# The first norm of a hybrid decoder layer: another way to start TensorE, another split of the first loads, and a small load issued later

## The chip, the core and the metric

The kernel runs on one core of one Trainium2 chip. The metric is the device time of one execution in microseconds (us); lower is better. The engines are TensorE (PE, with its weight loads shown apart as PEld), VectorE (DVE), ScalarE (ACT), GpSimd (POOL) and SyncE (SP). SP, ACT and POOL each have a queue from which they issue DMA transfers. Every engine works its own instructions off in order and waits on semaphores for the others.

## The reference, cut to what matters

One layer on x of shape (1, 512, 1024), all float32:

```
h    = rmsnorm(x, attn_norm_g)              # per row: x / sqrt(mean(x*x) + 1e-6) * g
proj = h @ w_in                             # 1024 -> 5144 columns: attention q, k, v, RWKV-7 inputs, gates
o_a  = nsa_mixer(...)                       # compressed, selected and windowed attention, 8 heads
o_b  = rwkv7_mixer(...)                     # recurrence over 512 tokens, 8 heads of 64
x    = x + (sigmoid(ga) * (o_a @ w_proj_a) + sigmoid(gb) * (o_b @ w_proj_b)) @ w_out
x    = x + conv_ffn(rmsnorm(x, ffn_norm_g)) # 1024 -> 2 x 2816 -> 1024
```

The compressed attention branch maps blocks of 32 tokens by a small two-layer network: `gelu(flat @ cmp_w1) @ cmp_w2`, once for keys (k) and once for values (v). `cmp_w1` is 2048 x 256, `cmp_w2` is 256 x 64.

## The kernel before

Every large product is computed from two float32r parts of each operand: a weight tile `raw` is loaded by SP's queue (line 267, 512 KB each as a rule, three buffers in turn), ACT rounds it to `whi` (`act`, line 124), DVE or POOL writes the rest `wlo` (line 296), and TensorE runs three products for each block of 128 inputs: hi\*hi, hi\*rest, rest\*hi (`mm`, line 121). The activations are kept the same way, as `hh` and `hl`, with channels on the partitions.

**The first norm** (lines 145 to 374) makes `hh` and `hl` from x. Its order on PE, ACT, DVE and POOL is written out by hand.

- x stands in four tiles `xt[:, t]` of 128 rows by 1024. SP issues their four loads first (line 153). ACT issues the load of the identity matrix (`ident`, in the tile `kc`, line 154) and of the norm's gains (`pr0`, line 155), POOL the loads of eight small parameter vectors into `pra` (line 162). Between, ACT takes one square root of a constant, which loads its table.
- PE runs 16 transposes of `ident` that nothing reads (line 329, `NWARM = 16`).
- For each tile t: ACT squares the row and sums it, ACT and DVE make the reciprocal root (`rstd1`, five small steps), DVE scales the tile into `hs[t]` (line 131). The last tile is scaled in two halves of 512 columns. PE then transposes the tile in blocks of 128 x 128 (`turn`, line 335) into eight PSUM banks `pts[k]`, one for each block k of channels; tile 2 leaves its last block, and tile 3 all of its blocks, to the loop below.
- After tile 1's transposes PE also transposes `pr0` and `pra` (lines 349 and 350) into a corner of bank 7. ACT copies the gains out as `ang`, DVE copies the rest as `prm` (line 353) and makes `omm = 1 - mu` from it.
- ACT rounds the first weight tile to `hi` before `ang`. POOL then writes one column of `omm` into `lo` (line 355), and after that the true `lo` in two halves (line 357). POOL's one-column copy is overwritten; it only makes POOL wait for `omm`.
- A loop over k transposes the rest of bank k, ACT writes `hh[:, k]` from it (a copy with a scale), and DVE writes `hl[:, k]`.
- The first product `p0` follows. Its bank is one of the four that `pts[0]` to `pts[3]` use, so it waits until DVE has read `pts[0]`.

**The compression** (function `compress`) runs in steps between the chunks of the RWKV recurrence, whose order on PE and SP is written out by hand; a scheduler orders ACT and DVE there. Each of four steps `s4` takes two tiles of `cmp_w1`, k and v, and multiplies them into `hx`. When `s4 == 1` is done SP issues the two loads of `cmp_w2` into `cw2` (line 805, 64 KB each, in rows of 256 bytes). `cw2` is read some steps later, by the second layer. In SP's queue these two loads stand between the loads of `cmp_w1` for `s4 == 2`, ahead of a tile of `w_in` and of the last k tile of `cmp_w1` (into `AB`).

Of the kernel before, what the change touches and what calls it, by code (L numbers as in the profile page):

```python
# [11 lines left out]
F32 = mybir.dt.float32  # L12
F32R = mybir.dt.float32r
I32 = mybir.dt.int32
AF = mybir.ActivationFunctionType
# [6 lines left out]
D = 1024  # L22
NT = S // 128
# [18 lines left out]
ROWS = {}  # L42
# [39 lines left out]
def hybrid_block(ctx: ExitStack, tc: tile.TileContext, A: dict, out: bass.AP):  # L82
    nc = tc.nc
    v, sc, te = nc.vector, nc.scalar, nc.tensor
    NWARM = 16

    def dbg(name, ap):
        if name in DBG:
# [2 lines left out]
    x_in = A["x"][0]  # L91
# [28 lines left out]
    def mm(o, l, r, start, stop):  # L120
        te.matmul(o, lhsT=l, rhs=r, start=start, stop=stop)  # L121

    def act(o, i, f=AF.Copy, **kw):
        sc.activation(o, i, f, **kw)  # L124
# [4 lines left out]
    def ts(o, a, s1, s2, op0=ALU.mult, op1=ALU.add):  # L129
        if s2 is None:  # L130
            v.tensor_scalar(o, a, s1, None, op0=op0)
        else:
            v.tensor_scalar(o, a, s1, s2, op0=op0, op1=op1)
# [6 lines left out]
    ident, mask, ones, cmask = kc[:, 0:128], kc[:, 128:256], kc[:, 256:384], kc[:, 384:416]  # L140
# [3 lines left out]
    xp_cm, xp = pool("x")  # L144
    xt = xp.tile([128, NT, D], F32, name="xt")
    eps1 = xp.tile([128, 1], F32, name="eps1")
    v.memset(eps1, 1e-6)
    one = xp.tile([128, 1], F32, name="one")
    v.memset(one, 1.0)
    act(one, one, AF.Sqrt)  # L150
    pr0 = xp.tile([8, 128], F32, name="pr0")
    for t in range(NT):
        nc.sync.dma_start(xt[:, t], x_in[128 * t:128 * t + 128])
    sc.dma_start(ident, A["consts"][:, 0:128])
    sc.dma_start(pr0, A["attn_norm_g"][0].rearrange("(r p) -> r p", p=128))
    pra = xp.tile([NR0, 128], F32, name="pra")
    for name in ("rwkv_mu", "rwkv_w0", "rwkv_a0", "rwkv_k_k", "rwkv_k_a", "rwkv_r_k", "rwkv_ln_g", "rwkv_ln_b"):
        r0, n = ROWS[name]
# [4 lines left out]
    ang = cp.tile([128, 8], F32, name="ang")  # L163
# [5 lines left out]
    def cols(name):  # L169
        r0, n = ROWS[name]  # L170
        return prm[:, r0:r0 + n]
# [154 lines left out]
    with tc.manual_schedule(engines={getattr(mybir.EngineType, e) for e in ("PE", "Activation", "DVE", "Pool")}):  # L326
        pts = [mmb() if k < 4 else pa() if k < 6 else pb() for k in range(KT)]
        for i in range(NWARM):
            te.transpose(pts[7][:, 384:512], ident, ident)
        hi = wp.tile([128, KT, 128], F32R, name="whi", tag="whi", bufs=2)  # L330
        lo = wp.tile([128, KT, 128], F32R, name="wlo", tag="wlo", bufs=2)
        raw = loads.pop(0)[0]

        def turn(t, k):
            te.transpose(pts[k][:, 128 * t:128 * t + 128], hs[t][:, 128 * k:128 * k + 128], ident)

        for t in range(NT):
            r = ssx[:, t:t + 1]
            act(hs[t], xt[:, t], AF.Square, accum_out=r)
            rstd1(r)  # L340
            for c0 in ((0, 512) if t == NT - 1 else (0,)):
                c1 = 512 + c0 if t == NT - 1 else D
                ts(hs[t][:, c0:c1], xt[:, t, c0:c1], r, None)
            if t < NT - 1:
                for k in range(KT - t // 2):
                    turn(t, k)
            if t == 1:
                pt = pts[7][:, 384:512]
                te.transpose(pt[:, 0:8], pr0, ident[0:8, 0:8])
                te.transpose(pt[:, 8:8 + NR0], pra, ident[0:NR0, 0:NR0])  # L350
        act(hi, raw)
        act(ang, pt[:, 0:8])
        v.tensor_copy(prm[:, 0:NR0], pt[:, 8:8 + NR0])
        ts(omm, cols("rwkv_mu"), -1.0, 1.0)
        nc.gpsimd.tensor_copy(lo[:, 0, 0:1], omm[:, 0:1])
        for i in (slice(0, 4), slice(4, 8)):
            nc.gpsimd.tensor_tensor(lo[:, i], raw[:, i], hi[:, i].bitcast(F32), op=ALU.subtract)
        late.append(nc.gpsimd.tensor_copy)
        wsplit()
        for k in range(KT):  # L360
            for t in range(NT - 1 - k // 7, NT):
                turn(t, k)
            act(hh[:, k], pts[k], AF.Copy, scale=ang[:, k:k + 1])
            stt(hl[:, k], pts[k], ang[:, k:k + 1], hh[:, k].bitcast(F32), ALU.mult, ALU.subtract)
        ts(w0h, cols("rwkv_w0"), 0.5, None)
        ts(kah, cols("rwkv_k_a"), 0.5, None)
        ts(a0h, cols("rwkv_a0"), 0.5, None)
        ts(oma, cols("rwkv_k_a"), -0.5, 1.0)
        p0 = mmb()
        for k in range(KT):  # L370
            mm(p0, hi[:, k], hh[:, k], k == 0, False)
            if k:
                mm(p0, lo[:, k - 1], hh[:, k - 1], False, False)
            mm(p0, hi[:, k], hl[:, k], False, False)
        mm(p0, lo[:, KT - 1], hh[:, KT - 1], False, True)
# [403 lines left out]
    def compress():  # L779
        Rk = [sg1[:, 2 * a:2 * a + 2].rearrange("p m s -> p (m s)").rearrange("p (j g n) -> p j g n", j=16, g=2)  # L780
              for a in range(2)]
        for a, s_ in enumerate("kv"):
            v.memset(Rk[a][:, :, :, 31:32], 0.0)
            r0 = ROWS["cmp_pe_" + s_][0]
            for g in range(2):
                dv = Dc[:, a, g].rearrange("p (n j) -> p j n", j=8)
                for jh in range(2):
                    tt(Rk[a][:, 8 * jh:8 * jh + 8, g, 0:31], dv[:, :, jh:31 + jh],
                       prm[:, r0 + 8 * jh:r0 + 8 * jh + 8, None].to_broadcast([128, 8, 31]), ALU.add)
        cw2, hid, hidT, kcd = (QK[:, o:o + 256] for o in range(3072, 4096, 256))  # L790
        cw2 = cw2.rearrange("p (a m d) -> p a m d", a=2, m=2)
        hidT = hidT.rearrange("p (m a n) -> p m a n", m=2, a=2)
        kcd = kcd[0:32].rearrange("p (g a d) -> p g a d", g=2, a=2)
        kcs = cp.tile([32, 2], F32, name="kcs")
        yield
        hx = mmb()[:, 0:256]
        for s4 in range(4):
            w = [wnext(4, 256) for _ in range(2)]
            for j in range(4):
                for a in range(2):  # L800
                    mm(hx[64 * a:64 * a + 64], Rk[a][:, 4 * s4 + j].rearrange("p g n -> p (g n)"), w[a][:, j],
                       s4 + j == 0, s4 + j == 6)
            if s4 == 1:
                for a, s_ in enumerate("kv"):
                    nc.sync.dma_start(cw2[:, a], A["cmp_w2_" + s_][0].rearrange("(m p) d -> p m d", p=128))
            yield
        act(hid, hx, AF.Square)
        ts(hid, hid, 0.044715, 1.0)
        tt(hid, hid, hx, ALU.mult)
        act(hid, hid, AF.Tanh, scale=math.sqrt(2.0 / math.pi))  # L810
        stt(hid, hid, 1.0, hx, ALU.add, ALU.mult)
        yield
        pt = mmb()
        for m in range(2):
            te.transpose(pt[:, 128 * m:128 * m + 128], hid[:, 128 * m:128 * m + 128], ident)
        act(hidT.rearrange("p m a n -> p (m a n)"), pt[:, 0:256])
        yield
        kc_ps = mmb()
        for g in range(2):
            for m in range(2):  # L820
                mm(kc_ps[0:32, 64 * g:64 * g + 64], hidT[:, m, 0, 32 * g:32 * g + 32], cw2[:, 0, m], m == 0, m == 1)
        nc.gpsimd.memset(vcb, 0.0)
        for g in range(2):
            for e in range(2):
                bs = slice(64 * g + 32 * e, 64 * g + 32 * e + 32)
                for m in range(2):
                    mm(kc_ps[bs, 128:192], hidT[:, m, 1, 32 * g:32 * g + 32], cw2[:, 1, m], m == 0, m == 1)
        for g in range(2):
            for e in range(2):
                bs = slice(64 * g + 32 * e, 64 * g + 32 * e + 32)  # L830
                act(vcb[bs, 2 * g + e], kc_ps[bs, 128:192], AF.Copy, scale=0.5)
        for g in range(2):
            act(kcd[:, g, 0], kc_ps[0:32, 64 * g:64 * g + 64], AF.Copy, scale=0.5)
            act(kcd[:, g, 1], kcd[:, g, 0], AF.Square, accum_out=kcs[:, g:g + 1])
        rstd(kcs, DH)
        for g in range(2):
            ts(kcd[:, g, 1], kcd[:, g, 0], kcs[:, g:g + 1], None)
            ts(kcd[:, g, 0], kcd[:, g, 0], kcs[:, g:g + 1], None)
        yield
        pt = mmb()  # L840
        for g in range(2):
            te.transpose(pt[:, 32 * g:32 * g + 32], kcd[:, g].rearrange("p a d -> p (a d)"), ident[0:32, 0:32])
        ptv = pt[:, 0:64].rearrange("p (g n) -> p g n", g=2)
        act(KC[:, :, 0], ptv, AF.Copy, scale=kg)
        stt(KC[:, :, 1], ptv, kg, KC[:, :, 0].bitcast(F32), ALU.mult, ALU.subtract)
# [530 lines left out]
```

## Time and profile before

| | us |
|---|---|
| runs | 837.89, 836.97, 837.40 |
| median of the runs | 837.40 |
| the profiled execution's own time | 838.0 |
| its span, first instruction to last | 836.2 |
| PE busy in the span | 822.0 |
| DVE, ACT, POOL busy | 515.8, 407.2, 51.5 |

The profile is that of one execution. Its times count from the first instruction; 1.8 us of the execution's own time lie outside the span. A row of the timeline gives the start, the duration and the engine of an instruction or of several equal ones in a row, the line of the kernel, and what is written from what; in square brackets stands how long the engine sat idle before it and what released it. L124, L121, L131, L133 and L136 are lines of one-line helpers (`act`, `mm`, `ts` without and with an addend, and `stt`), so such rows are told apart by their tiles. "Idle before" is shown only where there was some. The granted clock is 1.00 in every stretch that the profile lists, so the pace of TensorE in the first microseconds is read from the spacing of its rows.

### The profile page before, as it was taken

How to read it: one execution, taken by the hardware profiler on the slowest of the kernel's cores; microseconds unless marked ns; L12 is line 12 of the kernel's file. 1: busy time of each engine (PE TensorE's matmuls, PEld its weight loads, DVE VectorE, ACT ScalarE, POOL GpSimd, SP SyncE). 2: the span in 40 equal slices, each digit the busy share in tenths (PEclk: the TensorE clock that was granted, in tenths of full speed). 3: DMA queues.
4: the chain of work that ended last, by engine and by line, in shares of the span. 5: the costliest groups of instructions: out<-in, count | busy, mean ns of one | idle time of the engine just before them, and what ended most of it. 6: DMA issues, size and time to landing. Idle time of an engine off the chain costs nothing.

```text
span 836.2 us, 12860 instructions
## 1 busy us (share of the span) xinstructions
PE 822.0 (98%) x5091; PEld 668.2 (80%) x5091; DVE 515.8 (62%) x1003; ACT 407.2 (49%) x794; POOL 51.5 (6%) x68
## 2 busy tenths in 40 slices
PE   7999999999999999999999999999999999999998
PEld 6777778887778886777788988888888888888886
DVE  5477779974565878787665665566655566322222
ACT  6766654453455777676334454444444444221220
POOL 6200020140000100011000000000000000000000
PEclk9999999999999999999999999999999999999999
DMA  7432222346372310000275033333333332223421
GB/s 233 112 81 70 76 76 77 79 117 185 102 127 77 83 45 14 26 27 26 67 251 174 1 101 100 101 102 88 92 98 101 100 101 97 85 97 114 139 75 51
DMA packets 109264, 78.73 MB, mean 94 GB/s; under 512 B 3869, under 2 KB 97876, under 8 KB 109204
## 3 DMA queue, kind: packets, MB, share of 16 engines
q1 hardware_dynamic: 106800, 73.92, 30.6%
q10 hardware_dynamic: 1060, 2.55, 1.0%
q0 software_dynamic: 1344, 1.45, 0.8%
q8 instruction: 40, 0.66, 0.3%
q14 instruction: 20, 0.16, 0.1%
HBM read 74.56 MB, written 2.29 MB: 92 GB/s over the span
## 4 chain that ended last, share of the span: by engine, by line
PE 53%; DVE 0%; DVEq 0%; issue 0%
PE ps_mm L121 52%; PE ps_a L200 0%; PE ps_b L200 0%; PE ps_a L121 0%; PE ps_b L1180 0%; PE ps_mm L1180 0%; DVE x L127 0%; DVEq L1372 0%; PE ps_a L1132 0%
## 5 line engine op out<-in xcount | busy, mean ns | idle before, releaser
L121 PE MATMUL ps_mm<-hh,whi 128*128 128x512 f32 (+1 forms) x624 | 242.4, 391 | 1.4 <-DVE hl L136 0.8
L296 DVE TENSOR_TENSOR wlo<-raw,whi 128x1024 fp32r<-128x1024 f32 (+1 forms) x111 | 131.5, 1185 | 180.0 <-PE ps_mm L121 157.8
L121 PE MATMUL ps_mm<-hl,whi 128*128 128x512 f32 (+1 forms) x624 | 240.2, 387 | 0.0
L124 ACT ACTIVATE whi<-raw 128x1024 fp32r<-128x1024 f32 (+3 forms) x124 | 123.3, 996 | 155.9 <-PE ps_mm L121 142.1
L121 PE MATMUL ps_mm<-hh,wlo 128*128 128x512 f32 (+1 forms) x624 | 152.1, 384 | 0.0
L121 PEld LDWEIGHTS ps_mm<-hh,whi 128*128 128x128 f32 x624 | 117.2, 188 | 28.2 <-ACT whi L124 1.5
L121 PEld LDWEIGHTS ps_mm<-hl,whi 128*128 128x128 f32 x624 | 117.4, 188 | 23.0 <-issue 1.0
L121 PEld LDWEIGHTS ps_mm<-hh,wlo 128*128 128x128 f32 x624 | 115.1, 188 | 23.5
L121 PE MATMUL ps_mm<-whi,aT 128*128 128x512 f32 x352 | 84.5, 390 | 0.0
L121 PEld LDWEIGHTS ps_mm<-whi,aT 128*128 128x128 f32 x352 | 65.9, 188 | 14.3 <-issue 0.4
L136 DVE SCALAR_TENSOR_TENSOR cgv<-ps_mm,cw,cgv 128x511 f32<-128x511 f32 (+1 forms) x88 | 65.4, 746 | 1.6
L124 ACT ACTIVATE cgv<-ps_mm,cw 128x512 f32<-128x512 f32 x44 | 34.2, 780 | 23.3 <-PE ps_mm L121 23.3
L121 PE MATMUL ps_mm<-wlo,aT 128*128 128x512 f32 x176 | 44.3, 389 | 0.0
L124 ACT ACTIVATE P<-P,nm 128x512 f32<-128x512 f32 (+3 forms) x64 | 35.4, 553 | 15.0 <-DVE nm L1154 14.9
L124 ACT ACTIVATE aT<-cgv 128x512 fp32r<-128x512 f32 x22 | 13.9, 632 | 56.8 <-DVE cgv L127 56.8
L121 PEld LDWEIGHTS ps_mm<-wlo,aT 128*128 128x128 f32 x176 | 33.0, 188 | 6.9
L124 ACT ACTIVATE cgv<-cgv 128x512 f32<-128x512 f32 x22 | 13.9, 632 | 41.0 <-DVE cgv L136 41.0
L296 POOL TENSOR_TENSOR wlo<-raw,whi 128x512 fp32r<-128x512 f32 (+3 forms) x13 | 20.5, 1577 | 203.2 <-PE ps_mm L121 148.8
L1154 DVE CUSTOM_DVE_ANT_0 P<-ps_a,AB 128x512 f32<-128x512 f32 (+3 forms) x64 | 29.4, 484 | 4.2 <-PE ps_a L121 3.7
L127 DVE TENSOR_TENSOR x<-x,ps_mm 128x512 f32<-128x512 f32 (+1 forms) x17 | 11.1, 656 | 24.4 <-PE ps_mm L121 23.2
L127 DVE TENSOR_TENSOR aT<-cgv,aT 128x512 fp32r<-128x512 f32 x22 | 15.3, 693 | 14.7 <-ACT aT L124 14.7
L121 PE MATMUL ps_a<-KH,qst 128*128 128x512 f32 (+3 forms) x64 | 21.4, 349 | 1.6 <-DVE nm L1154 0.9
(354 smaller groups left out, 1202.1 us busy)
## 6 DMA issues: line engine op xcount, KB each, us to landing
raw<-in_w_up_dram SPq DMA_DIRECT2D x44, 512.0 KB, 3.8
raw<-in_w_in_dram SPq DMA_DIRECT2D x38, 512.0 KB, 4.1
raw<-in_w_down_dram SPq DMA_DIRECT2D x22, 512.0 KB, 3.6
raw<-in_w_out_dram SPq DMA_DIRECT2D x8, 512.0 KB, 4.1
xt<-in_x_dram SPq DMA_DIRECT2D x4, 512.0 KB, 5.3
raw<-in_cmp_w_v_dram SPq DMA_DIRECT2D x4, 512.0 KB, 3.9
raw<-in_w_proj_b_dram SPq DMA_DIRECT2D x8, 256.0 KB, 2.7
raw<-in_w_proj_a_dram SPq DMA_DIRECT2D x8, 256.0 KB, 2.7
```

The costliest lines, as they stand in the source:

```text
L121: te.matmul(o, lhsT=l, rhs=r, start=start, stop=stop)
L124: sc.activation(o, i, f, **kw)
L127: v.tensor_tensor(o, a, b, op=op)
L136: v.scalar_tensor_tensor(o, a, s, b, op0=op0, op1=op1)
L296: eng.tensor_tensor(lo, raw, hi.bitcast(F32), op=ALU.subtract)
L1154: v.tensor_tensor_reduce(out=P[:, i], in0=sp[:, N * (i - i0):N * (i - i0) + N], in1=BT[:, h, 384 - 128 * qt:512], scale=-1.0, scalar=-NEG, ...
```

## The change

- PE's start: a tile `warm` of 128 x 128 ones, filled by DVE, is multiplied with itself 15 times (plain float32 matmuls through `mm`) in place of the 16 transposes of `ident`.
- The first loads: the rows of tiles 0 and 1 are split in two halves of 64, SP loads the upper, ACT the lower. `ident` follows on ACT's queue behind its two halves, and `pr0` behind the square root. The order on ACT and SP is now written out by hand here too.
- The last tile is scaled in columns 0 to 255 and 256 to 1023.
- ACT makes `ang` ahead of `hi`. `omm` is made from the PSUM bank in place of `prm`. POOL's copy of `omm` into `lo` is gone.
- The compression issues the loads of `cw2` after step 2 in place of step 1. In SP's queue they stand now behind the `w_in` tile and behind the last k tile of `cmp_w1`.

In the built program PE's order is otherwise the same but for six matmuls of the second product, which come out in a slightly different order of hi and rest. At one place of the recurrence the scheduler now puts, on ACT, the rounding of a weight tile (`whi`) ahead of a gate (`sg`) and of the recurrence's `UV`; on DVE `wlo` now stands ahead of its copy to `UV`. Nothing else moves.

```
-    NWARM = 16
+    NWARM = 15
...
-    act(one, one, AF.Sqrt)
+    warm = xp.tile([128, 128], F32, name="warm")
+    v.memset(warm, 1.0)
     pr0 = xp.tile([8, 128], F32, name="pr0")
-    for t in range(NT):
-        nc.sync.dma_start(xt[:, t], x_in[128 * t:128 * t + 128])
-    sc.dma_start(ident, A["consts"][:, 0:128])
-    sc.dma_start(pr0, A["attn_norm_g"][0].rearrange("(r p) -> r p", p=128))
+    with tc.manual_schedule(engines={mybir.EngineType.Activation, mybir.EngineType.SP}):
+        for t in range(2):
+            nc.sync.dma_start(xt[0:64, t], x_in[128 * t:128 * t + 64])
+            sc.dma_start(xt[64:128, t], x_in[128 * t + 64:128 * t + 128])
+        for t in range(2, NT):
+            nc.sync.dma_start(xt[:, t], x_in[128 * t:128 * t + 128])
+        sc.dma_start(ident, A["consts"][:, 0:128])
+        act(one, one, AF.Sqrt)
+        sc.dma_start(pr0, A["attn_norm_g"][0].rearrange("(r p) -> r p", p=128))
...
         for i in range(NWARM):
-            te.transpose(pts[7][:, 384:512], ident, ident)
+            mm(pts[7][:, 384:512], warm, warm, True, True)
...
             act(hs[t], xt[:, t], AF.Square, accum_out=r)
             rstd1(r)
-            for c0 in ((0, 512) if t == NT - 1 else (0,)):
-                c1 = 512 + c0 if t == NT - 1 else D
+            cut = (0, 256, D) if t == NT - 1 else (0, D)
+            for c0, c1 in zip(cut, cut[1:]):
                 ts(hs[t][:, c0:c1], xt[:, t, c0:c1], r, None)
...
                 te.transpose(pt[:, 0:8], pr0, ident[0:8, 0:8])
                 te.transpose(pt[:, 8:8 + NR0], pra, ident[0:NR0, 0:NR0])
+        act(ang, pt[:, 0:8])
         act(hi, raw)
-        act(ang, pt[:, 0:8])
         v.tensor_copy(prm[:, 0:NR0], pt[:, 8:8 + NR0])
-        ts(omm, cols("rwkv_mu"), -1.0, 1.0)
-        nc.gpsimd.tensor_copy(lo[:, 0, 0:1], omm[:, 0:1])
+        r0, n = ROWS["rwkv_mu"]
+        ts(omm, pt[:, 8 + r0:8 + r0 + n], -1.0, 1.0)
         for i in (slice(0, 4), slice(4, 8)):
             nc.gpsimd.tensor_tensor(lo[:, i], raw[:, i], hi[:, i].bitcast(F32), op=ALU.subtract)
...
-            if s4 == 1:
+            if s4 == 2:
                 for a, s_ in enumerate("kv"):
                     nc.sync.dma_start(cw2[:, a], A["cmp_w2_" + s_][0].rearrange("(m p) d -> p m d", p=128))
```

## The prediction

> **What bounds the kernel now.** I read the page's busy times first, then the timeline of the first 15 us engine by engine, then TensorE's waits, and last the one stretch behind the norm in which a wait of TensorE meets the second edit.
>
> ```profile
> span 836.2 us, 12860 instructions
> PE 822.0 (98%) x5091; PEld 668.2 (80%) x5091; DVE 515.8 (62%) x1003; ACT 407.2 (49%) x794; POOL 51.5 (6%) x68
> ```
>
> TensorE is busy for 822.0 of 836.2 us, so nearly all that is left to win is the 14.2 us in which it is idle, and what it does at a slow pace or for nobody. The timeline of TensorE up to the first product:
>
> ```profile
> 4.85 3.67 PE L329 MATMUL ps_b<-kc 128*128 128x128 f32 x16 [4.85 <-DMA kc<-in_consts_dram]
> 8.31 1.06 PE L335 MATMUL ps_mm<-kc,h 128*128 128x128 f32 x4
> ...
> 10.02 1.06 PE L335 MATMUL ps_mm<-kc,h 128*128 128x128 f32 x4
> 10.87 0.42 PE L335 MATMUL ps_a<-kc,h 128*128 128x128 f32 x2
> ...
> 11.44 0.23 PE L349 MATMUL ps_b<-kc,pr 8*128 8x8 f32 x1
> ...
> 11.79 0.66 PE L335 MATMUL ps_mm<-kc,h 128*128 128x128 f32 x4
> ...
> 12.61 0.60 PE L335 MATMUL ps_mm<-kc,h 128*128 128x128 f32 x4
> ...
> 14.50 0.50 PE L121 MATMUL ps_mm<-hh,whi 128*128 128x512 f32 x1 [0.75 <-DVE hl L136]
> ```
>
> The reader is to see three things. The warm-up waits 4.85 us for the identity. It ends at 8.31. And the pace changes: 16 transposes from 4.85 to 8.31 are 0.216 us each, four from 10.02 to 10.87 still 0.21, but tile 2's seven from 11.79 to 12.61 take 0.117. So TensorE came to its full pace at about 10.9, 6.0 us after its first instruction, and most of the norm's transposes ran at half pace. From 14.50 on it hardly stops; what is won ahead of 14.50 should reach the end. The other engines in the same stretch:
>
> ```profile
> 4.65 1.06 ACT L124 ACTIVATE h<-xt 128x1024 f32<-128x1024 f32 x1 [1.95 <-DMA xt<-in_x_dram]
> ...
> 8.84 1.06 ACT L124 ACTIVATE h<-xt 128x1024 f32<-128x1024 f32 x1
> ...
> 10.03 0.29 ACT L124 ACTIVATE rx_y<-ssx,eps 128x1 f32<-128x1 f32 x1
> 10.43 1.06 ACT L124 ACTIVATE whi<-raw 128x1024 fp32r<-128x1024 f32 x1
> 11.89 0.18 ACT L124 ACTIVATE ang<-ps_b 128x8 f32<-128x8 f32 x1 [0.40 <-PE ps_b L350]
> 12.98 0.69 ACT L124 ACTIVATE hh<-ps_mm,ang 128x512 fp32r<-128x512 f32 x1 [0.91 <-PE ps_mm L335]
> ```
>
> ```profile
> 6.80 0.75 DVE L131 TENSOR_SCALAR h<-xt,ssx 128x1024 f32<-128x1024 f32 x1
> ...
> 8.17 0.75 DVE L131 TENSOR_SCALAR h<-xt,ssx 128x1024 f32<-128x1024 f32 x1
> ...
> 9.55 0.75 DVE L131 TENSOR_SCALAR h<-xt,ssx 128x1024 f32<-128x1024 f32 x1
> ...
> 11.00 0.88 DVE L131 TENSOR_SCALAR h<-xt,ssx 128x512 f32<-128x512 f32 x2
> 12.10 0.20 DVE L353 COPY prm<-ps_b 128x42 f32<-128x42 f32 x1 [0.22 <-ACT ang L124]
> ...
> 13.70 0.75 DVE L136 SCALAR_TENSOR_TENSOR hl<-ps_mm,ang,hh 128x512 fp32r<-128x512 f32 x1 [1.18 <-ACT hh L124]
> ```
>
> The scaled tiles 0, 1 and 2 are ready at 7.55, 8.92 and 10.30, the first half of tile 3 at 11.44. TensorE begins on tile 0 at 8.31, on tile 2 at 11.79, on tile 3 at 12.61: it is late for each. ACT waits for it 0.40 and 0.91 us, DVE then 1.18. TensorE's slow pace sets the start of `hh`, and by `hl` the start of the first product.
>
> **The start of TensorE.** The fill of `warm` is one DVE instruction of 128 columns, less than the 0.44 us of half a tile's scaling, so the first warm matmul starts at some 1.2 us. What a float32 matmul costs is seen here:
>
> ```profile
> 54.16 1.02 PE L121 MATMUL ps_a<-kk,kc 128*128 128x512 f32 x2
> 55.03 0.59 PE L121 MATMUL ps_a<-tv,kc 128*128 128x512 f32 x1
> ```
>
> One of 512 columns occupies 0.87 us, so 128 columns take 0.22 at full pace and 0.43 at half. Fifteen at half pace last 6.5 us, to 7.7; with the full pace after the same 6.0 us as before (at 7.2) they end at 7.5. Tile 0 is ready at 7.55. So the warm-up costs 0 to 0.15 us there, and the transposes run at 0.117: tile 0 to 8.6, tile 1 from 8.92 to 9.9, then the two small transposes, 0.35 from 11.44 to 11.79 before. These need the last of POOL's parameter loads:
>
> ```profile
> 4.97 0.51 POOL L162 DMA_DIRECT2D pra<-in_rwkv_ln_b_dram  x1
> ...
> 12.58 0.19 POOL L355 CAST wlo<-omm 128x1 fp32r<-128x1 f32 x1 [6.82 <-DVE omm L133]
> 12.85 1.27 POOL L357 TENSOR_TENSOR wlo<-raw,whi 128x512 fp32r<-128x512 f32 x1
> ```
> ```profile
> pra<-in_rwkv_ln_b_dram POOLq DMA_DIRECT2D x1, 2.0 KB, 4.9
> ```
>
> It lands at 4.97 + 4.9 = 9.9, just in time; that cover of 1.5 us is gone. `ang` follows ACT's last small step (10.03 + 0.29), at 10.35, then `hi`, 1.06, to 11.6. Tile 2 is transposed by 11.15. The first 256 columns of tile 3: 0.75 us for 1024 columns and 0.44 for 512 give about 0.29 for 256, so they are ready at 11.29; from TensorE's start on the block to ACT's `hh` were 12.98 - 12.61 = 0.37, which makes 11.7. So `hh` starts at 11.7, the later of 11.6 and 11.7, in place of 12.98: **1.28 us** earlier, and the first product at 14.50 - 1.28 = 13.2. The other piece (0.6) ends at 11.9, `prm` and `omm` (0.2 each) at 12.3, ahead of `hl` at 11.7 + 0.72 = 12.42. POOL's `lo` loses its dummy copy and starts with `hi`'s end at 11.6; its first half is done at 12.9, and the first product, which needs it after some matmuls, starts at 13.2 (below). As the first weight tile, `ang` and the last piece come within 0.2 us of each other and the latest one counts, I take **1.2**, with 0.1 (all of the delay was elsewhere) and 1.4 as the ends.
>
> **The split loads.**
>
> ```profile
> L153 SPq DMA_DIRECT2D xt<-in_x_dram x4: 382/422/546, 0.7 to 2.1; - x4
> ...
> DMA to landing us min/median/max: 3.9/5.3/6.7
> ```
>
> Tile 0 lands at 0.74 + 3.9 = 4.64, tile 3 at 2.1 + 6.7 = 8.8: 1.39 us a tile. ACT starts on them at 4.65 and 8.84, so both the landings and ACT's own pace hold it. The bytes ahead of tile 3 stay the same. Tile 0 no longer shares with `ident`, an eighth of a tile: 0.17 earlier at best; if ACT's half comes behind SP's by a whole issue (0.55 at most), that much later. ACT idled 1.95 us ahead of 4.65, so two more issues of 0.38 to 0.55 there, and `pr0` behind them, are covered. I take **0**, between -0.17 and +0.55, since tile 3 counts. [...]
>
> **The small load.** The stretch of the compression, ACT, DVE and TensorE:
>
> ```profile
> 197.70 0.60 ACT L124 ACTIVATE sg<-ps_mm 128x512 f32<-128x512 f32 x1 [6.21 <-PE ps_mm L121]
> ...
> 198.86 0.36 ACT L124 ACTIVATE UV<-ps_b 64x256 f32<-64x256 f32 x1
> 199.73 1.06 ACT L124 ACTIVATE whi<-raw 128x1024 fp32r<-128x1024 f32 x1 [0.51 <-DMA raw<-in_w_in_dram]
> ```
> ```profile
> 199.25 0.43 DVE L950 COPY UV<-ps_b 64x256 f32<-64x256 f32 x1 [4.08 <-ACT UV L124]
> 200.82 1.23 DVE L296 TENSOR_TENSOR wlo<-raw,whi 128x1024 fp32r<-128x1024 f32 x1 [1.14 <-ACT whi L124]
> ```
> ```profile
> 198.21 1.95 PE L121 MATMUL ps_mm<-raw,sg 128*64 128x256 f32 x16
> 200.84 0.50 PE L121 MATMUL ps_mm<-hh,whi 128*128 128x512 f32 x1 [0.68 <-ACT whi L124]
> ```
> ```profile
> 203.78 0.63 PE L121 MATMUL ps_a<-UV,BKT 128*64 128x64 f32 x14
> ```
>
> TensorE stands 0.68 us for `whi`, which stood for the landing of its raw tile. In the window from 194 to 195 the transfers were
>
> ```profile
> DMA packets 723, 0.30 MB, mean 298 GB/s; under 512 B 560, under 2 KB 723, under 8 KB 723
> ```
>
> and the 560 packets under 512 bytes are those of `cw2`: most of a microsecond of all 16 engines, ahead of that tile in the queue. Behind it, the tile lands up to 0.9 earlier, and `whi` ends by 200.16, where TensorE is ready. I take **0.65**, between 0 and 0.68. The new order of ACT and DVE costs nothing: even if the tile still came at 199.73, `whi`, `sg` and `UV` end at 201.8 on ACT, `wlo` and the copy to `UV` at 202.5 on DVE, and TensorE reads `UV` at 203.78. The last k tile of `cmp_w1` moves up too, and `cw2` itself is read much later.
>
> **The sum.** The profiled execution took 838.0. 838.0 - 1.2 - 0 - 0.65 = 836.2 (836.15 rounded). The median of the runs is 837.4, 0.6 lower. I read that as the moment of the full pace, which need not fall at 10.9 in each execution: an earlier one shortens the old norm and hardly the new one. [...]
>
> **Rivals.** *The profiled time is high for another reason.* Then the 0.6 comes off both kernels: 837.4 - 1.85 = 835.6. For it: no run shows the pace of the others. Against it: the lowest run, 836.97, is 1.0 below the profiled one, about what the norm alone could give. Chance 0.22.
>
> *The loads take over.* Tile 0 0.55 late carries ACT's whole chain along (8.84 - 4.65 = 4.19 for three tiles, with no slack in it), or `pra`, whose cover is gone, comes that late: 836.15 + 0.55 = 836.7. Chance 0.17.
>
> *The small load was not what delayed the tile*, or its wait turns up at the next step: 836.15 + 0.65 = 836.8. Chance 0.10.
>
> *TensorE falls back to half pace* (the other side). Between 7.5 and 13.2 it has 32 transposes of 0.117 and 0.35 of small ones, 4.1 of 5.7 us, with gaps between the tiles; before, it had no gap until after 13.5. If that is too little, the first products run at half pace until it is regained, for 6.0 us by the rows above, a loss of 3.0: 836.15 + 3.0 = 839.2. It decides if the loss of pace lasts beyond 1.9 / 0.5 = 3.8 us. Against it: transposes alone brought the full pace before. [...] Chance 0.09.
>
> **How the numbers follow.** The forecast, 836.2, has 0.42. A measurement can tell about 0.2% here, 1.7 us: faster is below 835.7, slower above 839.1. Faster: the rival of 835.6 (0.22), and the lower part of the forecast's own spread, 0.13. Slower: the fall of the pace and a little more, 0.11. Within: 0.54. The range reaches from 835.1 (the 835.6 with the better ends of the terms) to 837.6 (both load rivals together with a little of the norm's gain lost).
>
> **What would show it.** Right: the first PE row near 1.2, the spacing halved by 7.9, tile 0's transposes at 7.6, `hh` near 11.7, the first product near 13.2, no wait for `whi` in the step at 198 to 201. Wrong: a second slow stretch of matmuls after 8 us; ACT's first square after 4.7; `ang` waiting for `pra`; the 0.68 us still there, or at another step; or a median below 835.6, which would say that the profiled time was not the one to start from.

## The result, and the profile after

The changed kernel takes 839.61 us (median, 838.17 to 840.86) against 837.40 of the kernel before (836.97 to 838.11) in the same rounds: 1.0026 times as long, interval 1.0016 to 1.0037. The prediction was 836.2, between 835.1 and 837.6. The profiled execution took 839.77, so its trace stands for the median. First the page's span and busy times:

```profile
span 837.9 us, 12897 instructions
PE 824.1 (98%) x5105; PEld 670.0 (80%) x5105; DVE 515.9 (62%) x1004; ACT 406.5 (49%) x794; POOL 51.2 (6%) x67
```

TensorE is busy 2.1 us longer than before, and the span is 1.7 longer. Most of the extra busy time is the warm-up, which is now longer than the old one, so it says nothing yet about the loss. The timeline of TensorE up to the first product does:

```profile
1.12 5.28 PE L121 MATMUL ps_b<-warm 128*128 128x128 f32 x30 [1.12 <-DVE warm L151]
10.58 0.63 PE L341 MATMUL ps_mm<-kc,h 128*128 128x128 f32 x4 [4.18 <-DMA kc<-in_consts_dram]
...
11.48 1.05 PE L341 MATMUL ps_mm<-kc,h 128*128 128x128 f32 x4
...
13.51 0.33 PE L356 MATMUL ps_b<-kc,pra 42*128 42x42 f32 x1
13.78 1.11 PE L341 MATMUL ps_mm<-kc,h 128*128 128x128 f32 x4
...
15.12 0.60 PE L341 MATMUL ps_mm<-kc,h 128*128 128x128 f32 x4
...
17.02 0.50 PE L121 MATMUL ps_mm<-hh,whi 128*128 128x512 f32 x1 [0.75 <-DVE hl L136]
```

The warm-up does what was meant: it starts at 1.12. It ends at 6.40 and not at the 7.5 of the forecast: in this execution its matmuls halve their spacing near 4.8, some 3.7 us after the start and not 6.0 (the first 15 of the 30 end at 4.69, the other 15 at 6.40). Then TensorE stands for 4.18 us, and what ends the wait is the landing of the identity (`kc`), which before came at 4.85. The transposes start at full pace, four in (11.04 - 10.58) 0.46. At 11.48 they fall to half, four in 0.84, and they are back at full pace by 15.12. The first product starts at 17.02 where it was 14.50. Why it all comes late is seen on ACT, in its timeline with its queue:

```profile
0.75 1.47 ACTq L156 DMA_DIRECT2D xt<-in_x_dram  x2
2.26 0.60 ACTq L159 DMA_DIRECT2D kc<-in_consts_dram  x1
...
5.75 1.06 ACT L124 ACTIVATE h<-xt 128x1024 f32<-128x1024 f32 x1 [1.35 <-DMA xt<-in_x_dram]
...
8.16 1.06 ACT L124 ACTIVATE h<-xt 128x1024 f32<-128x1024 f32 x1 [0.93 <-DMA xt<-in_x_dram]
...
11.20 1.06 ACT L124 ACTIVATE h<-xt 128x1024 f32<-128x1024 f32 x1 [0.20 <-DMA xt<-in_x_dram]
...
13.88 0.18 ACT L124 ACTIVATE ang<-ps_b 128x8 f32<-128x8 f32 x1 [1.21 <-PE ps_b L356]
```

The squares of tiles 0, 1 and 3 start at 5.75, 8.16 and 11.20, in place of 4.65, 6.03 and 8.84, and each has waited for its load. Before, only that of tile 0 had; the rows of tiles 0 and 3 stand in the prediction, and that of tile 1 shows no idle time either:

```profile
6.03 1.04 ACT L124 ACTIVATE h<-xt 128x1024 f32<-128x1024 f32 x1
```

The DMA view from 1 to 11 us, of before and then of after (operation, count, size of one, median us from issue to landing):

```profile
xt<-in_x_dram SPq DMA_DIRECT2D x4, 512.0 KB, 5.3
...
kc<-in_consts_dram ACTq DMA_DIRECT2D x1, 64.0 KB, 4.1
```

```profile
xt<-in_x_dram SPq DMA_DIRECT2D x2, 512.0 KB, 7.5
xt<-in_x_dram SPq DMA_DIRECT2D x2, 256.0 KB, 4.7
xt<-in_x_dram ACTq DMA_DIRECT2D x2, 256.0 KB, 5.9
```

Half a tile takes about as long as a whole one did. The windows of 2 us (busy time of each engine, then the granted clock, the DMA engines' busy share and GB/s) say it directly, before:

```profile
4.00:6.00 2.00, 1.15 (x6) 1.16 (x7) 0.15 (x1) 1.32 (x3) 1.76 (x4) 1.00 1.04 413
6.00:8.00 2.00, 2.00 (x11) 2.00 (x10) 1.67 (x8) 1.97 (x5) 0.00 (x0) 1.00 1.03 399
```

and after:

```profile
4.00:6.00 2.00, 2.00 (x17) 2.00 (x16) 0.00 (x0) 0.64 (x3) 1.73 (x4) 1.00 1.03 221
6.00:8.00 2.00, 0.40 (x4) 0.21 (x2) 0.79 (x5) 1.20 (x3) 0.00 (x0) 1.00 1.01 242
8.00:10.00 2.00, 0.00 (x0) 0.00 (x0) 1.11 (x4) 1.81 (x4) 0.00 (x0) 1.00 1.06 387
...
12.00:14.00 2.00, 2.00 (x10) 1.56 (x9) 1.72 (x7) 0.76 (x5) 0.00 (x0) 0.50 1.17 294
```

All 16 DMA engines are busy (share 1.0), yet they move 221 and 242 GB/s while the halves of 64 rows are in flight, and 387 once whole tiles are. The last line shows the second part of the loss, a granted clock of 0.50: TensorE at half pace.

The small load did its part. After, ACT's rounding of the weight tile in the compression still waits for its raw tile:

```profile
201.06 1.06 ACT L124 ACTIVATE whi<-raw 128x1024 fp32r<-128x1024 f32 x1 [6.97 <-DMA raw<-in_w_in_dram]
202.03 0.58 ACT L124 ACTIVATE sg<-ps_mm 128x512 f32<-128x512 f32 x1
```

but it is now the first of ACT's steps there, 1.33 us later than before where the norm had lost 2.52, and TensorE's wait of 0.68 for `whi` is on no list of its waits any more. The balance of the two traces closes nearly: 2.52 lost by the first product and 0.68 won back make 1.84; measured are 839.77 - 838.0 = 1.77.

### The profile page after: what moved, and what is told of

The parts are those of the page before. It is cut to its first block, busy times and chain, and to the rows that moved or that the text cites. A ratio compares the mean times of both kernels' runs of the same rounds, so it can differ in the third digit from the quotient of the medians.

```text
span 837.9 us, 12897 instructions
## 1 busy us (share of the span) xinstructions
PE 824.1 (98%) x5105; PEld 670.0 (80%) x5105; DVE 515.9 (62%) x1004; ACT 406.5 (49%) x794; POOL 51.2 (6%) x67
## 4 chain that ended last, share of the span: by engine, by line
PE 53%; DVE 0%; DVEq 0%; issue 0%
PE ps_mm L121 52%; PE ps_a L206 0%; PE ps_b L206 0%; PE ps_a L121 0%; PE ps_b L1186 0%; PE ps_mm L1186 0%; DVE x L127 0%; DVEq L1378 0%; PE ps_a L1138 0%
```

## The experiments

The theory after this reading is A: a load onto 64 of the 128 partitions moves at about half the rate, whatever its queue. Its rivals are: two queues at once slow each other (B); the identity's late issue alone is the loss (C); the fall of TensorE's pace is the loss, and the loads matter only through it (D).

**The small load alone.** The kernel before with

```
-            if s4 == 1:
+            if s4 == 2:
```

> The kernel before with the later load of cw2 alone. Theory (the two cw2 loads delayed the w_in tile): the wait of 0.68 us for whi near 200 is gone and the time falls by 0.6 to 0.7 us, to about 836.75 where the kernel before has 837.4. Rival (the wait turns up elsewhere): no change within 0.2 us.

Measured: 836.49 (836.30 to 837.40), ratio 0.9987 (0.9978 to 0.9995); the wait for `whi` is gone. That is 1.2 below the 837.71 of before in the same rounds, more than 0.65, though the interval (0.4 to 1.8 us) holds 0.65. Its trace shows something else that the prediction had only assumed, on TensorE's timeline:

```profile
8.43 0.60 PE L335 MATMUL ps_mm<-kc,h 128*128 128x128 f32 x4
...
13.90 0.50 PE L121 MATMUL ps_mm<-hh,whi 128*128 128x512 f32 x1 [0.75 <-DVE hl L136]
```

With the same norm as before, tile 0's transposes run at full pace from 8.43, where in the profile of before the pace came at 10.9, and the first product is 0.6 earlier. The moment of the full pace differs between executions.

**All of the change but the split.** The changed kernel with whole tiles on SP and the identity first on ACT:

```
-        for t in range(2):
-            nc.sync.dma_start(xt[0:64, t], x_in[128 * t:128 * t + 64])
-            sc.dma_start(xt[64:128, t], x_in[128 * t + 64:128 * t + 128])
-        for t in range(2, NT):
+        for t in range(NT):
             nc.sync.dma_start(xt[:, t], x_in[128 * t:128 * t + 128])
```

> The changed kernel with the four x tiles loaded whole by SP and the identity first on ACT's queue, as before; all else of the change stays. Theory (the split of the loads is what cost): tiles land at 4.6 to 8.9 again, the first product starts near 13.2, and the time is 835.5 to 836.3. Rival (the warm-up on a filled tile does not hold TensorE's pace until the transposes, whatever the loads): a second slow stretch after 8 us, first product at 14.5 or later, 837.4 to 839.

Measured: 836.34 (836.15 to 836.48), ratio 0.9982 (0.9973 to 0.9991). The profiled execution, TensorE:

```profile
1.12 5.77 PE L121 MATMUL ps_b<-warm 128*128 128x128 f32 x30 [1.12 <-DVE warm L151]
7.90 0.66 PE L338 MATMUL ps_mm<-kc,h 128*128 128x128 f32 x4 [1.01 <-DVE rx_m L133]
...
13.63 0.50 PE L121 MATMUL ps_mm<-hh,whi 128*128 128x512 f32 x1 [0.50 <-DVE hl L136]
```

There is no wait for the identity and no slow stretch, and the first product starts at 13.63. The whole loss lies in how the first loads are laid out. By its median this version is below both kernels. Against the small load alone, 836.49 in the same rounds, its lead of 0.15 is not clear of noise: the two intervals overlap.

**The split alone.** The kernel before with the changed load block, old warm-up.

> The kernel before with the split loads alone, the identity behind them on ACT's queue. Theory (the loads are late, the identity lands near 10.5): the old warm-up, which needs the identity, starts at 10.5 in place of 4.85 and the first product comes 5 to 6 us later than at 14.50, so about 843. Rival (the split itself costs nothing, the pace of TensorE does): x tiles land as before and the loss stays under 1.5 us.

Measured: 843.28 (842.88 to 843.84), ratio 1.0064 (1.0051 to 1.0078).

```profile
10.19 3.68 PE L333 MATMUL ps_b<-kc 128*128 128x128 f32 x16 [10.19 <-DMA kc<-in_consts_dram]
...
15.37 1.03 PE L339 MATMUL ps_mm<-kc,h 128*128 128x128 f32 x4
16.22 0.40 PE L339 MATMUL ps_a<-kc,h 128*128 128x128 f32 x2
...
19.83 0.50 PE L121 MATMUL ps_mm<-hh,whi 128*128 128x512 f32 x1 [0.75 <-DVE hl L136]
```

The old warm-up can only begin with the identity, at 10.19, and the first product is 5.33 later than in the profile of before; the median rose by 5.57. The changed kernel is 2.2 above the one before, 2.9 without the 0.68 that the small load was worth in the traces: its new start hid about half of what the split does to the old one. It also shows again that transposes alone bring the full pace: it comes near 16.2, 6.0 us after the first of them.

**The identity first, the split kept.** The changed kernel with the identity issued ahead of ACT's halves.

> The changed kernel with the identity issued first on ACT's queue, ahead of its two halves of x; the x loads stay split. It parts the wait for the identity from the late x. Theory (x itself is late, tile 3 at about 11.2): tile 0 is transposed from 8.7, but the chain of the last tile still ends late; first product at 15.5 if the pace holds, so about 838.2, between the changed kernel and before. Rival (the wait for the identity was all of it): first product near 13.2, about 836.

Measured: 840.41 (839.33 to 840.93), ratio 1.0029 (1.0018 to 1.0039): a miss, and C falls. TensorE no longer stands for the identity but for the tiles, twice:

```profile
8.87 0.66 PE L341 MATMUL ps_mm<-kc,h 128*128 128x128 f32 x4 [2.70 <-DVE h L131]
...
11.59 1.11 PE L341 MATMUL ps_mm<-kc,h 128*128 128x128 f32 x4 [1.63 <-DVE rx_m L133]
...
17.54 0.61 PE L121 MATMUL ps_mm<-hh,whi 128*128 128x512 f32 x1
```

The first product came at 17.54, not near the 15.5 expected if the pace held: this execution has the longest slow stretch of all (below).

**The halves on one queue.** Both halves of both tiles on SP, the identity first on ACT.

> The changed kernel with the four half tiles of x (64 rows each) all on SP's queue, and the identity first on ACT's. It parts the halves from the second queue. Theory A (a load onto 64 of the 128 partitions moves at half rate, whatever queue it is on): x lands as late as with the split, tile 3 near 11.2, the rate from 3 to 7.5 us is about 225 GB/s, and the time is that of the split with the identity first, 839.5 to 840.5. Theory B (two queues on the same engines slow each other): x lands at 4.6 to 8.9 and the time is 836.0 to 836.6.

Measured: 839.37 (838.08 to 840.53), ratio 1.0020 (1.0010 to 1.0029), a little under the range of A. The rate stays low with one queue, so B falls:

```profile
4.00:6.00 2.00, 2.00 (x17) 2.00 (x16) 0.00 (x0) 0.17 (x1) 1.74 (x4) 1.00 1.06 223
6.00:8.00 2.00, 0.46 (x5) 0.27 (x3) 0.71 (x5) 1.28 (x3) 0.00 (x0) 1.00 1.02 257
```

And TensorE stands twice here too, for shorter:

```profile
8.80 0.66 PE L341 MATMUL ps_mm<-kc,h 128*128 128x128 f32 x4 [2.33 <-DVE h L131]
...
11.10 0.69 PE L341 MATMUL ps_mm<-kc,h 128*128 128x128 f32 x4 [1.21 <-DVE rx_m L133]
```

**Halves by columns.** Two queues again, each half of 128 rows by 512 columns, the identity behind them as in the change:

```
-            nc.sync.dma_start(xt[0:64, t], x_in[128 * t:128 * t + 64])
-            sc.dma_start(xt[64:128, t], x_in[128 * t + 64:128 * t + 128])
+            nc.sync.dma_start(xt[:, t, 0:512], x_in[128 * t:128 * t + 128, 0:512])
+            sc.dma_start(xt[:, t, 512:D], x_in[128 * t:128 * t + 128, 512:D])
```

> The changed kernel with tiles 0 and 1 cut in columns in place of rows: SP loads columns 0 to 511 of all 128 rows, ACT the rest, the identity behind them as in the change. Two queues and half tiles stay, but each load reaches all partitions. Theory A (half the partitions, half the rate): full rate again, over 350 GB/s from 4 us on, tile 3 lands by 9.0, the identity by 6.5, first product at 13.2 to 13.7, 836.0 to 836.6. Theory B (two queues): about 225 GB/s, as the change, 839 to 840.

Measured: 836.74 (836.24 to 837.45), ratio 0.9992 (0.9983 to 1.0002). The same bytes go by the same two queues in the same number of transfers, and the rate is back:

```profile
4.00:6.00 2.00, 2.00 (x12) 2.00 (x11) 0.17 (x2) 1.44 (x3) 1.74 (x4) 1.00 1.05 362
6.00:8.00 2.00, 1.00 (x9) 0.81 (x8) 1.69 (x7) 1.44 (x3) 0.00 (x0) 1.00 1.01 382
```

The 2.9 us between this and the changed kernel come with the 64 rows, directly or by what they delay. That 64 rows are half the partitions and that a transfer has half as many rows go together here; a load of every second row was not tried. The rate is as A said, the moments are not. The profiled execution, 837.45, is the slowest of its ten: tile 3's square starts at 10.15, released by the load that was expected by 9.0, and the first product at 14.73 (13.2 to 13.7). The identity still is what tile 0's transposes wait for, 2.3 us later than expected, but 1.8 us earlier than in the change:

```profile
8.76 0.63 PE L341 MATMUL ps_mm<-kc,h 128*128 128x128 f32 x4 [1.76 <-DMA kc<-in_consts_dram]
```

**Whole tiles on two queues.** Tile 1 whole on ACT, the identity behind it.

> The changed kernel with whole tiles: tile 1 on ACT's queue, tiles 0, 2 and 3 on SP's, the identity behind tile 1. Theory A (half the partitions): full rate, 836.0 to 836.8. Theory B (two queues): slow while both queues run, tile 0 after 5.2, time 838 or more.

Measured: 836.85 (836.74 to 837.13), ratio 0.9991 (0.9981 to 1.0000). 410 GB/s from 4 to 6 us; tile 0 at 5.42, the first product at 14.11. Whole tiles by two queues cost no rate, but tile 0, with tile 1 in flight beside it, came 0.5 later than with all four on SP (4.94), and the first product 0.5 later too. So one sign of B was there, tile 0 after 5.2; its time of 838 or more was not.

**A longer warm-up.** The changed kernel with `NWARM = 34`, which keeps TensorE busy until the identity has landed.

> The changed kernel with 34 warm matmuls in place of 15, so that TensorE stays busy until the identity lands near 10.5; the split stays. It takes away the fall to half pace and leaves the late loads. Theory (the late loads and the fall of the pace share the loss): no slow stretch after 10.5, first product near 15.6 in place of 17.0, so 838.2 where the change has 839.6. Rival (the fall of the pace is all): first product by 14.5, 837 or less. Other rival (the pace costs nothing, the late loads all): no change, 839.6.

Measured: 838.73 (838.47 to 839.18), ratio 1.0015 (1.0006 to 1.0024).

```profile
11.48 0.60 PE L341 MATMUL ps_mm<-kc,h 128*128 128x128 f32 x4
...
16.38 0.50 PE L121 MATMUL ps_mm<-hh,whi 128*128 128x512 f32 x1 [0.75 <-DVE hl L136]
```

The granted clock is 1.00 in every window up to the first product, and the median is 0.9 below the changed kernel's: that is what the fall of the pace is worth, less what this warm-up costs by ending at 11.48, 0.9 after the 10.58 at which the transposes began there. So 0.9 is the least that the fall is worth. An estimate of the most, from the rows of the changed kernel: its last tile is scaled from 13.36 on, its first piece by some 13.65, and with the 0.37 from there to `hh` that the prediction read, `hh` could have started near 14.0 in place of 15.49, 1.5 earlier. The rest of the loss, 838.73 against the 836.34 of whole loads, is there without any fall of the pace. So D holds for a part only, by these numbers the smaller one.

**The old start with whole loads.** The kernel with whole loads, but 16 transposes of the identity in place of the warm tile.

> The changed kernel with whole x loads and the identity first, as in the run of whole loads, but with the old start: 16 transposes of the identity in place of the 15 matmuls on the filled tile. It parts the new start from the rest. Theory (the moment at which TensorE reaches its full pace falls between some 8 and 11 us with the old start and sets the norm's end in the later cases): times spread over about 1 us, from 836.2 to 837.3, median 836.7, where the run of whole loads had 836.15 to 836.48. Rival (the start does not matter): 836.3 with the same narrow spread.

Measured: 836.80 (836.56 to 837.73), ratio 0.9994 (0.9985 to 1.0002); first product at 14.00. In its trace the full pace comes between 9.44 and 9.75, inside the expected 8 to 11. Between this and the new start with whole loads lie 0.46 us of medians, but the two intervals overlap (0.9973 to 0.9991 there), so that the new start is faster is likely and not shown. The runs spread over 1.17 us here, 1.10 with the small load alone and 0.33 with the new start. That is not the warm tile's doing alone: with the new start and the columns they spread over 1.21, with the identity later over 0.89, and with tile 1 on ACT over 0.39.

**The identity later.** Whole loads and new start, the identity on SP behind tile 1.

> The changed kernel with whole x loads, and the identity's load on SP's queue behind tile 1 in place of first on ACT's, since the filled tile makes TensorE start without it. Theory (tile 0 no longer shares with the identity and lands up to 0.2 to 0.3 us earlier, and ACT's chain with it): first product near 13.3, 836.0 to 836.2. Rival (tile 3's landing sets the end): no change, 836.3. It is also the candidate to beat both kernels.

Measured: 836.87 (836.51 to 837.40), ratio 0.9993 (0.9984 to 1.0002): a miss. Tile 0 came 0.5 earlier and its transposes with it (7.42), but two other things were late then:

```profile
10.67 0.23 PE L354 MATMUL ps_b<-kc,pra 42*128 42x42 f32 x1 [0.63 <-DMA pra<-in_rwkv_ln_b_dram]
```

TensorE waited for the last of POOL's small parameter loads, and tile 2, now behind the identity in SP's queue, came 0.5 later (ACT's square of it at 8.15 after a wait of 0.86, against 7.69). With whole loads the identity first has the lower median, by 0.53 us, though the two intervals overlap.

## Why the prediction was wrong

**The step that failed** is the term for the split loads: 0, between -0.17 and +0.55. Its premise was that the bytes ahead of tile 3 stay the same and so does the time. The bytes did; the rate did not. 1 MB onto 64 rows at a time moved at 221 to 257 GB/s with two queues and with one, the same 1 MB by columns at 362 to 382. The squares of tiles 0, 1 and 3 started 1.10, 2.13 and 2.36 later (5.75, 8.16 and 11.20), and the identity, behind its two halves, came 5.7 later. The profile of before had no large load onto half the partitions, but it had a warning in eight loads of 128 KB onto 16 partitions each, `AB<-vd`. Its DMA view shows them beside loads of twice the size onto all partitions (count, size of one, median us to landing):

```profile
raw<-in_w_proj_b_dram SPq DMA_DIRECT2D x8, 256.0 KB, 2.7
...
AB<-vd SPq DMA_DIRECT2D x8, 128.0 KB, 9.2
```

The landing time holds waiting in the queue too (3.9 to 6.7 us for the four equal tiles of x in the same trace), but the rate says the same: from 240 to 242 us, mostly these loads, the DMA engines moved 115 GB/s at a share of 1.17, and from 238 to 240, mostly weight tiles on all partitions, 291 at 1.14. Source and row size differ between the two, so this was a hint and no proof. In the windows from 4 to 8 us shown above the rate was 221 to 257 GB/s with x in halves of 64 rows, and 362 to 413 with each load of x on all 128 partitions. With both halves in flight it was 221 and 242, with the halves in turn 223 and 257, so being in flight together gained nothing here.

**The rival of the other side** (TensorE falls back to half pace, 839.2) came within 0.4 us of the result by another way, so its number is luck. I placed the fall among the gaps between the tiles, for 6.0 us of first products at a cost of 3.0. In fact it was a consequence of the loads, it lasted 3.4 us, in the changed kernel it slowed transposes alone, and it is worth between 0.9 and, by the estimate above, 1.5 of the 3.3 us that separate the changed kernel from whole loads.

**The rival of the loads** (836.7) named the right chain, tile 0 late and ACT's squares behind it, but priced it by one issue of 0.55, as the term did; and it did not ask what the identity waits for. The description of the change said it: the identity follows behind the halves. I had counted it as an eighth of a tile less for tile 0, and not as 1 MB ahead of a load on which TensorE waits. Even at the rate of the columns, 362 to 382 GB/s, it came some 4 us later than before (8.76 against 4.85).

**What held.** The warm-up started at 1.12 (said: 1.2). With whole loads the first product came at 13.63 (13.2; tile 0's square began at 4.94, 0.3 later than in the profile of before), and the kernel took 836.34 (836.2). The last agreement is partly luck. In the same rounds the small load alone took 1.22 us off the median of before, and all of the change but the split 1.37: that leaves 0.15 for the new start and the reordered norm, not clear of noise, where the term was 1.2. The small load's wait went, and nothing in the compression took its place; its size, 0.65, lies in the measured interval, at half of the measured median. No cost of the reordering on ACT and DVE is seen. `pra`, whose cover I had called gone, did come late where the tiles came early enough (0.63 with the identity later).

**The 0.6 between the profiled time and the median** I had read as the moment of the full pace. The trace of the small load alone shows that moment some 2.5 us earlier with an unchanged norm. The narrow spread with whole loads fits, but other runs with the new start spread as widely as the old, so it proves nothing. Part of the term of 1.2 was only the lateness of the profiled execution: against it, the first product came 0.87 earlier, against the execution with the small load alone, 0.27.

## What to carry to other kernels

Split a load by columns or by whole tiles, so that each part reaches all partitions: with the queues unchanged, columns in place of 64 rows were 2.9 us here. What a queue issues first should be what an engine waits for first: behind two halves of x, the small identity came 4 to 6 us later than where its queue issued it first (8.76 by columns and 10.58 in the change, against 4.85 before). And a warm-up has to reach the real work: one that ended 4.18 us ahead of it gave part of what it bought back, and one that ended 1.01 ahead of it did not.

## What the hardware showed that I had not expected

**The slow stretches lasted 3.41 us, or twice that.** Quarter-microsecond windows at the fall and the return, first of the changed kernel, then with the identity first, then with one queue (the granted clock is the third number from the end):

```profile
11.25:11.50 0.25, 0.25 (x5) 0.25 (x4) 0.21 (x2) 0.25 (x1) 0.00 (x0) 0.96 1.01 231
...
14.75:15.00 0.25, 0.25 (x3) 0.25 (x2) 0.00 (x0) 0.25 (x1) 0.00 (x0) 0.71 1.17 295
```

```profile
10.75:11.00 0.25, 0.00 (x0) 0.00 (x0) 0.22 (x1) 0.25 (x2) 0.00 (x0) 0.95 1.17 283
...
17.75:18.00 0.25, 0.25 (x2) 0.20 (x3) 0.25 (x1) 0.25 (x2) 0.25 (x2) 0.89 0.00 0
```

```profile
11.50:11.75 0.25, 0.25 (x4) 0.25 (x3) 0.21 (x2) 0.25 (x1) 0.00 (x0) 0.69 1.21 291
...
15.00:15.25 0.25, 0.25 (x5) 0.25 (x4) 0.00 (x0) 0.15 (x1) 0.25 (x1) 0.98 1.20 306
```

Every other such window of the three traces between 10.50 and 19.00 reads 1.00 or 0.50. Taking the change as a step between the two, the share of each mixed window gives an estimate of the moment: 0.96 means 0.02 us of half pace at the end of its window, a fall at 11.48; 0.71 means 0.145 at the beginning of its own, a return at 14.895. The slow stretches are 3.41, 6.83 (10.975 to 17.805) and 3.41 (11.595 to 15.01): one, two and one of the same length. In the 3.41 us ahead of the fall TensorE had stood 2.5, 2.3 and 1.8 us (with one queue 8.18 to 8.80, the end of its gap of 2.33, and the 1.21 ahead of 11.10). With a single gap of 1.76 (columns) it kept its pace. So the fall did not need a gap as long as the slow stretch: with one queue it came after gaps of 2.33 and 1.21 us. Where the limit lies, and whether it is a limit on idle time at all, was not tried. The time from TensorE's first matmul to the full pace differs too. With the old start it was 6.0 us in the profile of before, at most 3.3 with the small load alone (5.17 to 8.43) and about 4.5 on whole loads (5.12 to between 9.44 and 9.75). The warm tile's start shows the same: it begins at 1.12 each time, and its 15 matmuls took from 5.05 to 5.88 us in seven traces, where the forecast had 6.3. No run shows what sets the moment.

**The granted clock does not show the slow beginning.** It stands at 1.00 while the old warm-up's transposes take 0.216 each, and at 0.50 for nearly the same spacing, 0.21, after a fall (from 11.48 in the changed kernel). Only the spacing tells the first.

**Two halves on two queues did not add up.** They go to different partitions by different queues, but together they moved no faster than four halves in turn on one queue (221 and 242 GB/s against 223 and 257). In the trace of the change the packets of the two queues took 60.6 and 38.8 per cent of the 16 engines' time from 4 to 8 us, so the engines worked for both queues, and were full. Why a packet then takes so long was not tried.
